# In-projection of a hybrid attention/HGRN2/Fourier layer: the split weights kept in DRAM by the first block of tokens, and one ring of seven buffers

## The chip, the cores and the metric

The kernel runs on one core of one Trainium2 chip. The metric is the device time of one execution in microseconds; lower is better.

## The reference

One layer of a diffusion backbone over 2048 latent tokens and 256 context tokens, width 1024, all in float32:

```python
p = modulate(x, norm1_g[l], sh1, sc1) @ w_in[l]
pc = modulate(ctx, norm1_g[l], csh1, csc1) @ w_in[l]
# columns of p: latent attention (queries, keys/values, rotary key) | HGRN2 (q, two gates, input, output gate) | Fourier
y = jnp.concatenate([attn, hg, fn], axis=-1) @ w_out[l]
x_new = x + g1 * y
x_new = x_new + g2 * swiglu_ffn(modulate(x_new, norm2_g[l], sh2, sc2), w_gate_up[l], w_down[l])
return rms_norm(x, final_norm_g)
```

The change is in the first two lines: the in-projection, a product of the normalised tokens with `w_in` (1024 rows, 2752 columns).

## The kernel before

A product in full precision is made from parts: each operand is split into a high part (a rounded copy in the format float32r) and a low part (the operand less its high part), and three matmuls are added up in PSUM: high by low, high by high, low by high (`mm3`, lines 83 to 85). The helper `hi` makes a high part on POOL (line 72), on ACT (line 74) or on DVE; `lo` makes a low part on DVE (line 79).

The in-projection is the first large stage of the kernel, from about 30 to 895 us. It goes over the context block (256 tokens) and then over four blocks of 512 tokens. In each block, the columns of `w_in` are taken in groups: values and output gate (`values_in`, 512 columns), four heads of the HGRN2 recurrence (`head_in`, 384 columns each: q and two gates), attention (`attention_in`, 448 columns) and Fourier (`fourier_in`, 256 columns). Each group is cut along the 1024 rows into pieces of up to 128 x 1536 elements (`pieces`): three for values, two for each head, three for attention, two for Fourier, 16 in a block of 512 tokens. The context block has 14 pieces with other widths.

For each piece `load_w` loads the raw weights with one DMA on SP's queue per range of columns (line 244; a head's piece has three ranges of 128 columns), makes the high part on POOL (in the context block on ACT) and the low part on DVE, and the matmuls of the piece follow. Raw weights have three buffers (`wraw`), high parts two (`wh`), low parts two (`wl`), each of 128 x 1536 elements. The weights are the same for all blocks, and each block loads and splits them anew.

Between the groups stands the recurrence of each head (`hgrn`): the gates go through ACT (sigmoids, lines 363 and 364, 372), POOL (lines 367, 368, 370, 419), DVE (lines 375, 377, 413, 416) and ACT (copy `ku`, line 387), and PE multiplies small blocks of 128 columns (`psl`, line 392; `pfin`, lines 403 to 410). The gates' results are stored by SP from a ring of two buffers (`gt`), the Fourier part from another of two (`uv`).

The order of the instructions on each engine is laid down when the kernel is built, by the planner of the tile framework, which interleaves the matmuls of the next group with the small matmuls of the recurrence. On the chip each engine and each DMA queue works through its list in order, and waits at an instruction whose input or buffer is not ready.

Of the kernel before, what the change touches and what calls it, by code (L numbers as in the profile page):

```python
# [10 lines left out]
F32 = mybir.dt.float32  # L11
F32R = mybir.dt.float32r
# [7 lines left out]
P = 128  # L20
# [5 lines left out]
TB = 512  # L26
# [16 lines left out]
def tile_backbone(  # L43
# [6 lines left out]
    pe, act, dve, pool, sp = nc.tensor, nc.scalar, nc.vector, nc.gpsimd, nc.sync  # L50

    dram = ctx.enter_context(tc.tile_pool(name="dram", bufs=1, space=DRAM))
# [17 lines left out]
    def hi(eng, dst, src):  # L70
        if eng is pool:
            pool.tensor_scalar(dst, src, 1.0, 0.0, ALU.mult, ALU.add)  # L72
        elif eng is act:
            act.copy(dst, src)  # L74
        else:
            dve.tensor_copy(dst, src)

    def lo(dst, src, h, eng=None):
        (eng or dve).tensor_tensor(dst, src, h, ALU.subtract)  # L79

    def mm3(ps, ah, al, bh, bl, first, last, more=False):

        pe.matmul(ps, ah, bl, start=first, stop=False, skip_group_check=more)  # L83
        pe.matmul(ps, ah, bh, start=False, stop=False, skip_group_check=more)  # L84
        pe.matmul(ps, al, bh, start=False, stop=last, skip_group_check=more)  # L85
# [135 lines left out]
    with p1 as ph:  # L221
        e2 = ph.enter_context(tc.tile_pool(name="p1e2", bufs=2, reuse_waits="tile"))
        ea = ph.enter_context(tc.tile_pool(name="p1ea", bufs=1, reuse_waits="tile"))
        wp = ph.enter_context(tc.tile_pool(name="p1w", bufs=2, reuse_waits="tile"))
# [12 lines left out]
        early = {}  # L237

        def load_raw(cols, n, k0, nk):
            raw = wp.tile([P, 1536], F32, tag="wraw", bufs=3, name="wraw")  # L240
            rv = raw[:, :nk * n].rearrange("p (k n) -> p k n", k=nk)
            o = 0
            for s, wd in cols:
                sp.dma_start(rv[:, :, o:o + wd],
                             w_in[0, k0 * P:(k0 + nk) * P, s:s + wd].rearrange("(k p) n -> p k n", p=P))
                o += wd
            return raw

        def pieces(n):
            step = min(4, 1536 // n)  # L250
            return [(k0, min(step, KT - k0)) for k0 in range(0, KT, step)]

        for k0, nk in pieces(256):
            early[((C_HI, 256), k0)] = load_raw([(C_HI, 256)], 256, k0, nk)
# [4 lines left out]
            state[h] = b2.tile([P, 64], F32, tag=f"S{h}", bufs=6, name=f"S{h}_i")  # L259
            dve.memset(state[h], 0.0)  # L260

        def load_w(cols, n, k0, nk, eng):

            raw = early.pop((cols[0], k0), None)
            if raw is None:
                raw = load_raw(cols, n, k0, nk)
            wh = wp.tile([P, 1536], F32R, tag="wh", name="wh")
            wl = wp.tile([P, 1536], F32R, tag="wl", name="wl")
            hi(eng, wh[:, :nk * n], raw[:, :nk * n])
            lo(wl[:, :nk * n], raw[:, :nk * n], wh[:, :nk * n])  # L270
            return (wh[:, :nk * n].rearrange("p (k n) -> p k n", k=nk),
                    wl[:, :nk * n].rearrange("p (k n) -> p k n", k=nk))

# [44 lines left out]
        def token_major(xm, blk, cols):  # L318
            T = blk[3]
            n = sum(wd for _, wd in cols)  # L320
            acc = [psm.tile([P, 512], F32, tag="mm", name="acc") for _ in range(T // P)]
            for k0, nk in pieces(n):
                wh, wl = load_w(cols, n, k0, nk, pool if T == TB else act)
                for t in range(T // P):
                    for k in range(nk):
                        kk = k0 + k
                        ts = slice(t * P, (t + 1) * P)
                        mm3(acc[t][:, :n], xm[0][kk][:, ts], xm[1][kk][:, ts], wh[:, k, :], wl[:, k, :],
                            kk == 0, kk == KT - 1)
            return acc  # L330

        def feature_major(xm, blk, cols):
            T = blk[3]
            n = sum(wd for _, wd in cols)
            acc = [psm.tile([P, TB], F32, tag="mm", name="accf") for _ in range(n // P)]
            for k0, nk in pieces(n):
                wh, wl = load_w(cols, n, k0, nk, pool if T == TB else act)
                for f in range(n // P):
                    for k in range(nk):
                        kk = k0 + k  # L340
                        fs = slice(f * P, (f + 1) * P)
                        mm3(acc[f][:, :T], wh[:, k, fs], wl[:, k, fs], xm[0][kk][:, :T], xm[1][kk][:, :T],
                            kk == 0, kk == KT - 1)
            return acc
# [110 lines left out]
        def fourier_in(xm, blk):  # L455
            acc = feature_major(xm, blk, [(C_FN, 256)])
            zh = e1.tile([P, 2, TB], F32R, tag="zh", name="zh")
            zl = e1.tile([P, 2, TB], F32R, tag="zl", name="zl")
            for f in range(2):
                hi(act, zh[:, f, :], acc[f])  # L460
                lo(zl[:, f, :], acc[f], zh[:, f, :])
            for t in range(4):
                ts = slice(t * P, (t + 1) * P)
                pu = psm.tile([P, 512], F32, tag="mm", name="pu")
                for f in range(2):
                    mm3(pu, zh[:, f, ts], zl[:, f, ts], cwh[:, f, :], cwl[:, f, :], f == 0, f == 1)
                uv = e1.tile([P, 512], F32, tag="uv", bufs=2, name="uv")
                act.copy(uv, pu)
                sp.dma_start((uva[blk[4]] if blk[4] < NB - 1 else uvz)[t * P:(t + 1) * P, :], uv)

        def attention_in(xm, blk):
            _, w, t0, T, bi = blk
            lat = w == 0
            nt = T // P
            c0 = 0 if lat else C_CKV
            acc = token_major(xm, blk, [(c0, 448 - c0)])
            pt = ea.tile([P, 4, 448], F32, tag="pt", name="pt")
            sq = e2.tile([P, 2, 4], F32, tag="sq", name="sq")
# [70 lines left out]
        def values_in(xm, blk, vp):  # L549
            _, w, t0, T, bi = blk  # L550
            nt = T // P
            acc = token_major(xm, blk, [(C_HI, 512 if w == 0 else 256)])
            vt = vp.tile([P, 4, 256], F32, tag="vt", name="vt")
            for t in range(nt):
                dve.tensor_copy(vt[:, t, :], acc[t][:, 0:256])
                if w == 0:
                    gt = hp[0].tile([P, 256], F32, tag="gt", bufs=2, name="gt")
                    act.activation(gt, acc[t][:, 256:512], AF.Sigmoid)
                    dve.tensor_tensor(gt, acc[t][:, 256:512], gt, ALU.mult)  # L559
                    sp.dma_start(gates[bi][t * P:(t + 1) * P, :], gt)  # L560
            return vt

        def head_in(xm, blk, h):
            cols = [(C_HFF + h * P, P), (C_HFB + h * P, P)]
            if blk[1] == 0:
                cols = [(C_HQ + h * P, P)] + cols
            return feature_major(xm, blk, cols)
# [60 lines left out]
    with ExitStack() as ph:  # L628
# [377 lines left out]
        for b in range(NB):  # L1006
# [19 lines left out]
            if nxt is not None:  # L1026
                _, per_head, heads = nxt
# [10 lines left out]
    with ExitStack() as ph:  # L1038
        wr = ph.enter_context(tc.tile_pool(name="p5w", bufs=2, reuse_waits="tile"))
        wp = ph.enter_context(tc.tile_pool(name="p5p", bufs=9, reuse_waits="tile"))  # L1040
# [272 lines left out]
        for i, (s, j) in enumerate(units):  # L1313
# [4 lines left out]
            for o, n in enumerate(ORDER):  # L1318
# [15 lines left out]
                elif n == 7:  # L1334
                    f = f32("f", 2)
# [61 lines left out]
        for b in range(NB):  # L1397
            sq = b1.tile([P, 4, 2], F32, tag="sq7", bufs=2, name="sq7")
            rs = b1.tile([P, 4, 2], F32, tag="rs7", bufs=2, name="rs7")
            for c in range(2):  # L1400
                acc = [bank("dn") for _ in range(4)]
                for g, (k0, nk) in enumerate(DG):
# [7 lines left out]
                    w = wd.parts.pop(i)  # L1410
# [62 lines left out]
```

## Time and profile before

| what | value |
| --- | --- |
| time, median of 3 runs | 3324.02 us (3322.12 to 3328.81) |
| the profiled execution's own time | 3332.05 us |
| its span, first to last instruction | 3330.3 us |
| PE busy (matmuls) | 3166.0 us, 95% |
| DVE, ACT, POOL busy | 2131.1, 952.4, 1038.6 us |
| moved by DMA | 382.03 MB, 115 GB/s on the mean |

The profiled execution took 3332.05 us, 1.75 us more than its span and 8.0 us more than the median of the three runs. A line of a view names the source line (L79), the engine, the operation, what it writes and reads, and how often it stands there. PE is TensorE's matmuls, DVE VectorE, ACT ScalarE, POOL GpSimd, SP the engine that issues most DMAs.

### The profile page before, as it was taken

The numbers are of one execution on the slowest core, as the hardware profiler recorded it, in microseconds if no ns is written. First come the engines' busy times: TensorE is split into PE (matmuls) and PEld (weight loads), VectorE is DVE, ScalarE is ACT, GpSimd is POOL, SyncE is SP. The second block draws the span as 40 slices with busy tenths as digits, with TensorE's granted clock in tenths as the row PEclk, the third lists the DMA queues.
The fourth block names the chain that finished last, engine by engine and source line by source line (L and its number), as shares of the span: only waits on it lengthen the run. The fifth ranks groups of instructions, "written<-read, shape, count | busy, mean of one in ns | idle before, by whom it ended". The sixth has DMA issues, their size and how long they took to land. (4 is left out here: it accounts for less than half of the span.)

```text
span 3330.3 us, 45440 instructions
## 1 busy us (share of the span) xinstructions
PE 3166.0 (95%) x17034; PEld 2649.5 (80%) x17034; DVE 2131.1 (64%) x3211; ACT 952.4 (29%) x2028; POOL 1038.6 (31%) x1241
## 2 busy tenths in 40 slices
PE   7898989999879999999999989999999999999998
PEld 5777777777668888888888767888878888888886
DVE  6575665646776667676666367766776666555543
ACT  3222121222225555555553241111121111212111
POOL 3443452524430121121001443333333333243442
PEclk9999999999989999999999999999999999999999
DMA  6523233143361112120106665422342232664552
GB/s 228 165 70 124 80 104 92 55 117 102 114 186 34 51 49 79 55 69 26 36 32 228 221 218 161 142 76 86 113 134 80 77 95 92 212 211 155 177 171 70
DMA packets 354000, 382.03 MB, mean 115 GB/s; under 512 B 46234, under 2 KB 236532, under 8 KB 352756
## 3 DMA queue, kind: packets, MB, share of 16 engines
q1 hardware_dynamic: 339140, 368.11, 35.2%
q10 hardware_dynamic: 13776, 8.92, 0.8%
q8 instruction: 135, 2.21, 0.3%
q0 software_dynamic: 864, 2.10, 0.2%
q14 instruction: 85, 0.70, 0.1%
HBM read 293.33 MB, written 85.72 MB: 114 GB/s over the span
## 5 line engine op out<-in xcount | busy, mean ns | idle before, releaser
L72 POOL TENSOR_SCALAR wp<-wr 128x512 fp32r<-128x512 f32 x208 | 170.4, 835 | 354.5 <-PE dn L85 234.0
L890 DVE TENSOR_REDUCE mx<-sc 128x1 f32<-128x512 f32 (+1 forms) x320 | 201.9, 632 | 121.9 <-PE sc L888 121.1
L83 PE MATMUL dn<-wp,hdh 128*128 128x512 f32 x704 | 273.9, 389 | 0.0
L84 PE MATMUL dn<-wp,hdh 128*128 128x512 f32 x704 | 273.9, 389 | 0.0
L85 PE MATMUL dn<-wp,hdl 128*128 128x512 f32 x704 | 273.9, 389 | 0.0
L79 DVE TENSOR_TENSOR wp<-wr,wp 128x512 fp32r<-128x512 f32 x208 | 170.8, 859 | 138.9 <-POOL wp L72 138.7
L79 DVE TENSOR_TENSOR ptl<-ptv,pth 128x512 fp32r<-128x512 f32 x288 | 196.4, 686 | 67.3 <-ACT pth L74 65.0
L74 ACT CAST pth<-ptv 128x512 fp32r<-128x512 f32 x288 | 169.7, 593 | 234.1 <-PE ptv L904 223.7
L896 ACT ACTIVATE p<-sc,mx 128x512 f32<-128x512 f32 (+1 forms) x320 | 201.9, 649 | 91.9 <-DVE mx L893 87.7
L83 PE MATMUL y<-xol,wp 128*128 128x512 f32 x528 | 208.7, 395 | 9.8 <-ACT e L1325 4.6
L72 POOL TENSOR_SCALAR wp<-wg 128x512 fp32r<-128x512 f32 x176 | 131.6, 749 | 269.9 <-PE y L85 107.2
L84 PE MATMUL y<-xoh,wp 128*128 128x512 f32 x528 | 206.9, 392 | 0.0
L85 PE MATMUL y<-xoh,wp 128*128 128x512 f32 x528 | 206.6, 392 | 0.0
L79 DVE TENSOR_TENSOR wl<-wraw,wh 128x1536 fp32r<-128x1536 f32 (+3 forms) x78 | 118.7, 1522 | 119.6 <-POOL wh L72 117.0
L85 PE MATMUL accf<-xh,wl 128*128 128x512 f32 x448 | 184.6, 412 | 10.4 <-DVE wl L79 10.4
L888 PE MATMUL sc<-kth,q 128*128 128x512 f32 (+1 forms) x640 | 194.4, 377 | 0.0
L888 PE MATMUL sc<-kp,q 128*128 128x512 f32 (+1 forms) x640 | 190.0, 373 | 0.0
L83 PE MATMUL accf<-xl,wh 128*128 128x512 f32 x448 | 183.9, 410 | 0.4 <-DVE gt L559 0.4
L84 PE MATMUL accf<-xh,wh 128*128 128x512 f32 x448 | 183.1, 409 | 0.0
L79 DVE TENSOR_TENSOR wp<-wg,wp 128x512 fp32r<-128x512 f32 x176 | 128.5, 733 | 84.6 <-POOL wp L72 80.8
L904 PE MATMUL ptv<-ident,p 128*128 128x128 f32 x1152 | 179.1, 275 | 1.8 <-ACT p L896 1.8
L72 POOL TENSOR_SCALAR wp<-ws 128x512 fp32r<-128x512 f32 x132 | 90.2, 683 | 290.0 <-PE z L85 160.8
(367 smaller groups left out, 8426.4 us busy)
## 6 DMA issues: line engine op xcount, KB each, us to landing
wg<-in_w_gate_up_dram SPq DMA_DIRECT2D x88, 512.0 KB, 4.1
wr<-in_w_down_dram SPq DMA_DIRECT2D x40, 1024.0 KB, 5.3
wraw<-in_w_in_dram SPq DMA_DIRECT2D x112, 256.0 KB, 3.7
hr<-hid SPq DMA_DIRECT2D x88, 256.0 KB, 3.1
wm<-in_w_mod_dram SPq DMA_DIRECT2D x64, 256.0 KB, 2.8
hid<-f SPq DMA_DIRECT2D x44, 256.0 KB, 3.0
hid<-e SPq DMA_DIRECT2D x44, 256.0 KB, 2.0
wt<-in_w_mod_dram SPq DMA_DIRECT2D x8, 1024.0 KB, 7.7
```

The source lines that it names most:

```text
L72: pool.tensor_scalar(dst, src, 1.0, 0.0, ALU.mult, ALU.add)
L74: act.copy(dst, src)
L79: (eng or dve).tensor_tensor(dst, src, h, ALU.subtract)
L83: pe.matmul(ps, ah, bl, start=first, stop=False, skip_group_check=more)
L84: pe.matmul(ps, ah, bh, start=False, stop=False, skip_group_check=more)
L85: pe.matmul(ps, al, bh, start=False, stop=last, skip_group_check=more)
L888: pe.matmul(s[:, :n], a[:, ts], bb[:, js], start=i == 0, stop=i == 4)
L890: dve.tensor_reduce(mx[:, j:j + 1], s[:, :n], AX.X, ALU.max)
L896: act.activation(u["p"][:, a:e], u["s"][i][:, :e - a], AF.Exp, bias=mx[:, 5:6], accum_out=mx[:, 6 + i:7 + i])
L904: pe.transpose(pt[:, i, u * P:(u + 1) * P], ps[u]["p"][:, (2 * g + i) * P:(2 * g + i + 1) * P], ident)
```

## The change

The first block of tokens (T is 512, nothing kept yet) makes both parts of a piece as before and also stores them into two DRAM tensors of its own. The three later blocks load both parts with two DMAs of 128 rows, each row up to 6144 contiguous bytes, and make nothing. The context block has T = 256 and works as before. Raw weights, high parts and low parts share one ring of seven buffers where they had three, two and two of the same size.

```diff
         def load_raw(cols, n, k0, nk):
-            raw = wp.tile([P, 1536], F32, tag="wraw", bufs=3, name="wraw")
+            raw = wp.tile([P, 1536], F32, tag="w", bufs=7, name="wraw")
...
-        def load_w(cols, n, k0, nk, eng):
-
-            raw = early.pop((cols[0], k0), None)
-            if raw is None:
-                raw = load_raw(cols, n, k0, nk)
-            wh = wp.tile([P, 1536], F32R, tag="wh", name="wh")
-            wl = wp.tile([P, 1536], F32R, tag="wl", name="wl")
-            hi(eng, wh[:, :nk * n], raw[:, :nk * n])
-            lo(wl[:, :nk * n], raw[:, :nk * n], wh[:, :nk * n])
+        kept = {}
+
+        def load_w(cols, n, k0, nk, T):
+            at = (cols[0], n, k0)
+            have = kept.get(at)
+            raw = None
+            if have is None:
+                raw = early.pop((cols[0], k0), None)
+                if raw is None:
+                    raw = load_raw(cols, n, k0, nk)
+            wh = wp.tile([P, 1536], F32R, tag="w", bufs=7, name="wh")
+            wl = wp.tile([P, 1536], F32R, tag="w", bufs=7, name="wl")
+            if have is None:
+                hi(pool if T == TB else act, wh[:, :nk * n], raw[:, :nk * n])
+                lo(wl[:, :nk * n], raw[:, :nk * n], wh[:, :nk * n])
+            else:
+                for x, d in zip((wh, wl), have):
+                    sp.dma_start(x.bitcast(F32)[:, :nk * n], d)
+            if have is None and T == TB:
+                kept[at] = [dram.tile([P, nk * n], F32, name=f"w{x}{cols[0][0]}_{k0}") for x in "hl"]
+                for x, d in zip((wh, wl), kept[at]):
+                    sp.dma_start(d, x.bitcast(F32)[:, :nk * n])
```

In `token_major` and `feature_major` the call `load_w(cols, n, k0, nk, pool if T == TB else act)` becomes `load_w(cols, n, k0, nk, T)`.

## Rows read from the trace of the kernel before

**Rows 1.** The page's engines: busy us (share of the span) xinstructions.
```profile
PE 3166.0 (95%) x17034; PEld 2649.5 (80%) x17034; DVE 2131.1 (64%) x3211; ACT 952.4 (29%) x2028; POOL 1038.6 (31%) x1241
```
**Rows 2.** Windows: start, block 0, block 1; the sum is blocks 1 to 3.
```profile
core 0: us, PE busy (x) PEld busy (x) DVE busy (x) ACT busy (x) POOL busy (x), PEclk, DMA share, GB/s
24.00:32.00 8.00, 5.19 (x12) 0.67 (x10) 7.30 (x7) 0.44 (x1) 0.00 (x0) 1.00 0.99 349
105.00:310.00 205.00, 184.17 (x1095) 152.52 (x1094) 134.40 (x176) 57.81 (x121) 91.85 (x88) 0.98 0.41 123
310.00:505.00 195.00, 179.62 (x1105) 148.91 (x1104) 121.48 (x155) 45.90 (x91) 79.03 (x76) 0.97 0.31 91
...
sum 585.00, PE 545.98 PEld 453.08 DVE 361.71 ACT 129.43 POOL 232.31; mean PE 181.99 PEld 151.03 DVE 120.57 ACT 43.14 POOL 77.44
```
**Rows 3.** PE's waits, 310 to 895 us: total us, times, longest.
```profile
PE psl L392 <- ACT ku L387: 16.4, 10, 2.5
PE psl L392 <- DVE q L416: 9.1, 10, 1.8
PE accf L85 <- DVE wl L79: 6.9, 2, 3.5
PE pfin L408 <- DVE q L416: 3.7, 5, 0.9
```
**Rows 4.** Timeline of PE in block 1: start, duration, instruction, [idle before, releaser].
```profile
361.77 1.59 PE L392 MATMUL psl<-q,ku 128*128 128x128 f32 x8 [2.47 <-ACT ku L387]
...
426.28 1.59 PE L392 MATMUL psl<-q,ku 128*128 128x128 f32 x8 [1.54 <-ACT ku L387]
...
484.83 0.50 PE L85 MATMUL accf<-xh,wl 128*128 128x512 f32 x1 [3.46 <-DVE wl L79]
...
499.67 0.71 PE L392 MATMUL psl<-q,ku 128*128 128x128 f32 x3 [1.78 <-DVE q L416]
```
**Rows 5.** Timelines of POOL and (last row) DVE before 426 us.
```profile
415.23 0.77 POOL L367 TENSOR_SCALAR f<-f,omlb,lbt 128x512 f32<-128x512 f32 x1 [9.23 <-ACT f L363]
...
419.35 1.48 POOL L72 TENSOR_SCALAR wh<-wraw 128x1536 fp32r<-128x1536 f32 x1 [2.66 <-PE accf L84]
420.81 2.37 POOL L367 TENSOR_SCALAR f<-f,omlb,lbt 128x512 f32<-128x512 f32 x1
423.26 2.08 POOL L368 TENSOR_SCALAR k<-f 128x1024 f32<-128x1024 f32 x1
...
420.86 1.76 DVE L79 TENSOR_TENSOR wl<-wraw,wh 128x1536 fp32r<-128x1536 f32 x1 [1.37 <-POOL wh L72]
```
**Rows 6.** Timelines of POOL and DVE before 485 and before 500 us.
```profile
475.54 1.06 POOL L72 TENSOR_SCALAR wh<-wraw 128x1024 fp32r<-128x1024 f32 x1 [3.82 <-PE acc L85]
...
483.57 1.21 DVE L79 TENSOR_TENSOR wl<-wraw,wh 128x1024 fp32r<-128x1024 f32 x1
...
495.35 1.91 POOL L72 TENSOR_SCALAR wh<-wraw 128x1536 fp32r<-128x1536 f32 x1
...
494.84 2.96 DVE L79 TENSOR_TENSOR xl<-xmt,xh 128x512 fp32r<-128x512 f32 x2 [0.38 <-POOL xh L72]
```
**Rows 7.** Windows: the 6 us behind PE's stop at 361.77.
```profile
362.00:368.00 6.00, 5.79 (x25) 4.68 (x25) 4.72 (x5) 1.90 (x3) 4.85 (x8) 0.72 0.04 11
```
**Rows 8.** Windows of tile wh alone: what reads or writes it.
```profile
310.00:895.00 585.00, 341.59 (x1056) 198.37 (x1056) 72.94 (x46) 0.00 (x0) 65.44 (x46) 0.98 0.30 88
```
**Rows 9.** DMA issues: KB each, median us to landing.
```profile
wraw<-in_w_in_dram SPq DMA_DIRECT2D x8, 768.0 KB, 4.4
```
**Rows 10.** Timeline of PE: one matmul after another.
```profile
107.62 0.40 PE L83 MATMUL acc<-wl,xh 128*128 128x512 f32 x1
107.85 0.39 PE L84 MATMUL acc<-wh,xh 128*128 128x512 f32 x1
```
**Rows 11.** SP's own waits, 310 to 895 us.
```profile
SPq L244 <- DVE wl L79: 341.5, 33, 19.4
```
**Rows 12.** Windows: the start of block 0.
```profile
105.00:120.00 15.00, 12.31 (x67) 10.04 (x66) 8.68 (x16) 4.41 (x16) 6.28 (x7) 1.00 0.60 164
120.00:140.00 20.00, 19.61 (x87) 15.93 (x86) 12.15 (x18) 7.55 (x15) 7.16 (x7) 1.00 0.95 304
```

More of the change, by code (lines that the diff above doesn't have):

```diff
@@ L322, in token_major @@
             for k0, nk in pieces(n):
-                wh, wl = load_w(cols, n, k0, nk, pool if T == TB else act)
+                wh, wl = load_w(cols, n, k0, nk, T)
                 for t in range(T // P):
@@ L336, in feature_major @@
             for k0, nk in pieces(n):
-                wh, wl = load_w(cols, n, k0, nk, pool if T == TB else act)
+                wh, wl = load_w(cols, n, k0, nk, T)
                 for f in range(n // P):
```

## The prediction

> **What bounds the kernel now.** I read the page's table of engines first. PE is busy 3166.0 of the 3330.3 us, DVE 64%, POOL 31% [rows 1], so an edit pays only where it fills a gap on PE or where PE's clock rises. The change touches the in-projection alone, so I read that stage next, in windows: the context block up to about 105 us, the first block of tokens (block 0) from 105 to 310, blocks 1 to 3 from 310 to 895 [rows 2]. In blocks 1 to 3 PE is busy 545.98 of 585 us. Its idle time there is 39 us: all that can be won there besides the clock. DVE is busy 361.71 us, POOL 232.31, and in block 1 DMA is at 0.31 of its share. So no engine but PE is a bound, and what counts is whose result PE waits for.
>
> PE's waits in those three blocks [rows 3] answer that: 16.4 us for ACT's copy ku, 9.1 + 3.7 for DVE's q, 6.9 for wl, the low part of a weight. Only 6.9 names the removed work. The other waits have to be followed back one engine.
>
> **ku.** PE's longest stop of this kind in block 1 is 2.47 us, and the same stop comes again in blocks 2 and 3 [rows 4]. POOL's timeline before a second stop of the kind, the 1.54 us in rows 4, shows the cause [rows 5]: the sigmoid's L367 takes 0.77 us by itself; the next one stands behind a 1.48 us split of a weight (L72, high part) and itself takes 2.37 us, while DVE makes the low part of that weight (1.76 us, L79). Then POOL's k (2.08), then ACT's ku, then PE. So the split puts 1.48 + (2.37 - 0.77) = 3.08 us into the chain that PE waits for, at the stops of 2.47 and of 1.54 us alike; the ten stops of this kind are 16.4 us.
>
> **wl.** The 3.46 us stop at 484.83, and its twin in block 2 [rows 4]: POOL had the high part done at 476.6, but DVE reached the low part at 483.57, behind the attention part's normalisations [rows 6]. The weight was late only because DVE takes its work in order.
>
> **q.** The 1.78 us stop at 499.67, with a twin in block 2, follows two xl that took 2.96 us together while POOL ran a 1.91 us high part [rows 4, 6]. So 3.6 of the 12.8 us stand behind split work; the other stops are of 1.2 us and less, and I did not follow each.
>
> **The clock.** In the 6 us after the 2.47 us stop the granted clock is 0.72 against 0.97 over the block [rows 2, 7], and PE works at full speed again behind them, so such a stop costs a further 6 x 0.28 = 1.7 us. I take the same for the 3.46 us stops. That makes five (2.47 in each block, 3.46 in two): 8.4 us.
>
> **The change part by part.**
>
> *Removed, blocks 1 to 3:* 16 pieces in each block, so 48 high parts on POOL and 48 low parts on DVE; the trace holds 46 of each, 65.44 and 72.94 us [rows 8]. Neither engine is a bound, so these 138 us count for nothing by themselves; what counts is the waits above. (1) wl: 6.9 us, all of it, because the loaded parts need neither POOL nor DVE. (2) ku: 16.4 us stand behind split work that goes whole. But the instruction order is laid out anew when the kernel is built, and PE's psl will stand earlier once the plan thinks ku earlier; what remains of the chain (k alone is 2.08) can still be late. Bounds 0 and 16.4; I take two thirds, 11. (3) q: bounds 0 and 12.8; 4.5, the 3.6 that were followed back and a little of the rest. (4) Clock: 8.4 if all five stops go, 0 if none; with the two wl stops sure and two thirds of the others, 6. Sum 28.4, bounds 6.9 (wl alone) and 39 + 8.4 = 47 (no idle time left).
>
> On (2) a page can be weighed. Row: the POOL instruction beside DVE's two-input subtraction goes from 0.77 to 2.37 us, and DVE's subtraction is no longer than elsewhere [rows 5]. The Trainium skill (SBUF — State Buffer, Who interferes with whom) has it that a DVE instruction with two SBUF inputs and a GpSimd instruction that reads SBUF exclude each other for a whole instruction. By that, the 1.60 us vanish whole, all 16.4 us go, and the sum would be 5.4 us better; by the row with a new order it is the 11 I keep. The trace agrees with the blocking, though here the instruction that began first was the one held.
>
> *Moved onto DMA, blocks 1 to 3:* per block 2752 columns x 1024 rows x 4 B = 11.3 MB of raw weights become 22.5 MB of two parts. Block 1 moves 91 GB/s x 195 us = 17.7 MB [rows 2]; after, 29 MB, 148 GB/s. The highest rate in these rows is 349 GB/s at a share of 0.99, so the mean fits more than twice over. The number of issues on SP stays: 32 loads for 32 (3 + 4 x 2 x 3 + 3 + 2). A 768 KB load landed in 4.4 us [rows 9]; two for a piece are at most 9 us. With seven buffers and two per piece a load may start when the matmuls four pieces (high part) or three pieces (low part) before are done. A piece of 36 matmuls at 0.23 us is 8.3 us of PE [rows 10], on average 190 / 16 = 12 with the recurrence (the HGRN work of a head). So a load has two pieces, 16 to 24 us, to land in: cost nothing, covered by those matmuls. If that cover were gone it would be 4 us a piece. A load that waits for a buffer holds what stands behind it on SP: gates, mlap, uv and x. SP waits for wl in front of L244 already now, 341.5 us in these blocks [rows 11], without PE stopping for it.
>
> *Added, block 0:* 32 stores, 22.5 MB, on SP. Mean rate 123 GB/s plus 110 = 233, below 349. But from 120 to 140 us the queue is full: 304 GB/s at a share of 0.95 [rows 12]. From 105 to 140 it moves 8.5 MB and could move 12.2; the stores due there are the three pieces of the values (4.2 MB) and the first head piece (1.5). That is 2 MB too much, 6 us until there is room after 140. What waits is the raw load of the first head's second piece and the gate stores, whose two buffers hold ACT and so PE's accumulators. Bounds 0 and 6 + 1.7 of clock; I take 4.5. SP's store also waits for DVE's low part with raw loads behind it; those loads have two pieces to land in, as above.
>
> *The ring, context block and block 0:* a raw weight had a buffer when the low part three pieces earlier was made; now it needs the buffer of the low part three pieces back, so matmuls stand between. The context block's 14 pieces fill the 75 us before 105, 5.4 us each. Load, split and subtraction are at most 4.4 + 1.48 + 1.76 = 7.6 us by rows of larger pieces, against 10.8 us of two pieces: covered on the mean, with little to spare at the start. Bounds 0 and 5; I take 1.5. Behind the stage, the next stage's tiles lie where the ring lay and can be held until the last matmuls: no row here prices that, so 0, with -5 and +5 as an estimate, inside the range.
>
> *Sum:* -28.4 + 4.5 + 1.5 = -22.4. The profiled execution took 3332.05 us, span 3330.3 and 1.75 around; it becomes 3309.6. The median of the three runs is 8.0 lower, 3324.02, so I forecast 3302 there.
>
> **The rivals.**
>
> *All gaps close* (chance 0.07). For it: every long stop in blocks 1 to 3 was traced to split work. Against: k, kd and q still hinder each other on POOL and DVE. -47 + 4 = -43: 3281.
>
> *New waits for old* (0.15). The new order packs PE closer, so that the chain of the recurrence is late again by what the plan does not know, and only wl and its clock are won: -6.9 - 3.4, against 6 to 10 us lost in block 0 and the context: 3320 to 3324. For it: of q's 12.8 us only 3.6 were traced to split work. This is what holds most of "same".
>
> *Slower: the ring gives block 0 only one piece of lead* (0.13). SP keeps its order, so a raw load behind the stores of the piece before waits until that piece's low part is made, then lands behind two stores of some 4.4 us: 3 x 4.4 + 1.5 + 1.76 = 16.5 us after the matmuls that free it, against 8.3 us of PE for a piece with no recurrence beside it. At the six pieces of values and attention that is 6 x 8.2 = 49 us: 3324 - 28 + 49 = 3345. It decides from the point where a raw load has less than two pieces to land. Against it: only two of seven buffers hold a piece that the matmuls are at. Half the effect would end at 3321.
>
> *Bytes for arithmetic does not pay* (0.03). If the weights of blocks 1 to 3 came at the rate of the queue, they would need 29 MB / 349 GB/s = 83 us a block, below the 190 that PE needs, so they cannot bind on the mean. If the 34 MB more were exposed, they would cost 97 us: 3393 with what is won. The Trainium skill (SBUF — State Buffer, A bandwidth-pool intuition that's wrong) says that HBM is almost always the end-to-end bottleneck; the windows of this stage do not show it.
>
> That nothing changes because the parts are made anew each time is excluded: columns, width and first row of a piece are the same in all four blocks, and the context block, which has other widths, keeps nothing.
>
> **How the numbers follow.** My case, -8 to -40, has 0.62, so 3284 to 3316. About 0.2%, 6.6 us, is what a measurement of this kernel can tell from no change. Faster: 0.62 + 0.07 + 0.01 of the new waits = 0.70; same 0.13; slower 0.13 + 0.03 + 0.01 = 0.17. The range runs from the near end of "all gaps close", 3284, to 3328, which takes in new waits and the start of the slower case; outside are some 0.06 below and 0.12 above.
>
> **What would show it.** Right: in blocks 1 to 3 no L72 or L79 on weights, PE's waits for wl gone, those for ku under half, L367 near 0.77 us, PE's granted clock up from 0.97, each block some 8 to 10 us shorter; block 0 longer by a few us with about 230 GB/s. Wrong: PE waiting for a load of wh or wl in blocks 1 to 3, block 0 longer by over 15 us with PE waiting for wl or wraw, or ku waits unchanged though L367 is short.

## The result and the profile after

The changed kernel took 3362.3 us (median of 4 runs, 3356.95 to 3370.6) beside 3325.65 us for the kernel before on the same chip: ratio 1.0109, 95% interval 1.0094 to 1.0124. It is slower by 1.1%, where 0.7% faster was forecast; the time lies above the range. The profiled execution took 3366.77 us, its span is 3365.0 us, 34.7 us more than that of before.

The page's engines of the changed kernel first (busy us, share of the span, instructions; [rows 1] of before):

```profile
PE 3188.9 (95%) x17034; PEld 2668.9 (79%) x17034; DVE 2037.4 (61%) x3163; ACT 950.1 (28%) x2028; POOL 946.7 (28%) x1193
```

The arithmetic is gone as foreseen: DVE lost 93.7 us and POOL 91.9, in 48 instructions each. PE has the same instructions, but is busy 22.9 us longer, at a mean granted clock of 0.971 where before had 0.981.

To find the place of a loss I took two instructions that every block has, and read their first starts in the views by source line: the sigmoid of block 0's output gates on ACT (`gt`), which follows block 0's first group of matmuls (values and output gate), and the copies `uv`, which end each block. Before first, then the changed kernel, where lines stand 15 further down (the gates, then the end of block 0 and the end of block 3):

```profile
L558 ACT ACTIVATE gt<-acc x16: 384/385/387, 131.1 to 735.8; 128x256 f32<-128x256 f32 x16
...
L468 ACT COPY uv<-pu x4: 565/582/587, 304.5 to 308.2; 128x512 f32<-128x512 f32 x4
...
L468 ACT COPY uv<-pu x4: 586/586/591, 893.6 to 899.3; 128x512 f32<-128x512 f32 x4
```
```profile
L573 ACT ACTIVATE gt<-acc x16: 384/385/388, 158.4 to 759.0; 128x256 f32<-128x256 f32 x16
...
L483 ACT COPY uv<-pu x4: 587/588/592, 332.3 to 337.2; 128x512 f32<-128x512 f32 x4
...
L483 ACT COPY uv<-pu x4: 586/586/587, 920.4 to 929.5; 128x512 f32<-128x512 f32 x4
```

The 34.7 us are made up so: 27.3 us are lost before block 0's gates (158.4 against 131.1), 0.5 in the rest of block 0 (173.9 against 173.4), 1.0 is won in blocks 1 to 3 (588.1 against 589.1, from block 0's first `uv` to block 3's), and 7.9 are lost from there to the end (2444.6 against 2436.7). Of the 27.3 us, 21.7 are there at PE's first matmul of block 0 (128.5 us against 106.9).

**Blocks 1 to 3.** Windows of tile wh there (columns as in [rows 2]; [rows 8] of before), then the whole stage, then PE's waits ([rows 3] of before):

```profile
337.00:922.00 585.00, 349.00 (x1056) 202.97 (x1056) 0.00 (x0) 0.00 (x0) 0.00 (x0) 0.95 0.42 142
```
```profile
337.00:922.00 585.00, 551.41 (x3341) 458.54 (x3340) 273.28 (x417) 130.25 (x261) 146.98 (x180) 0.95 0.42 142
```
```profile
PE psl L407 <- ACT ku L402: 15.4, 10, 1.7
PE psl L407 <- DVE q L431: 11.9, 14, 1.6
PE ptx L312 <- ACT xmt L314: 5.3, 2, 2.8
```

No engine splits a weight any more, wl's 6.9 us are gone, and no kept load stands among the waits. But ku kept 15.4 of 16.4 us, q has 11.9 where 12.8 were, a new 5.3 us has come, and the clock of the stretch is 0.95 where three blocks of before had 0.98. Was the chain behind ku not shortened? It was. POOL, PE and the granted clock at the first stop of this kind in block 1 (timelines, then windows; [rows 4, 5, 7] of before):

```profile
380.38 0.77 POOL L382 TENSOR_SCALAR f<-f,omlb,lbt 128x512 f32<-128x512 f32 x1 [1.25 <-ACT f L379]
381.23 2.08 POOL L383 TENSOR_SCALAR k<-f 128x1024 f32<-128x1024 f32 x1
```
```profile
384.24 1.58 PE L407 MATMUL psl<-q,ku 128*128 128x128 f32 x8 [1.66 <-ACT ku L402]
388.38 2.05 PE L407 MATMUL psl<-q,ku 128*128 128x128 f32 x8 [1.06 <-DVE q L431]
418.54 1.57 PE L407 MATMUL psl<-q,ku 128*128 128x128 f32 x8 [1.40 <-ACT ku L402]
422.44 2.05 PE L407 MATMUL psl<-q,ku 128*128 128x128 f32 x8 [0.71 <-DVE q L431]
```
```profile
384.00:390.00 6.00, 4.70 (x19) 3.87 (x20) 4.76 (x4) 1.97 (x4) 5.30 (x8) 0.66 0.12 49
...
418.00:424.00 6.00, 4.74 (x19) 3.85 (x20) 4.98 (x4) 2.27 (x4) 5.55 (x6) 0.67 0.22 90
...
452.00:458.00 6.00, 4.44 (x19) 3.63 (x20) 4.91 (x4) 2.12 (x4) 5.45 (x8) 0.69 0.07 20
```

The first row is what a sigmoid's follow-up costs now: 0.77 us. The view by source line has it for all 24 of them in blocks 1 to 3 (least, median, greatest in ns), where the same view of the kernel before gave 768, 1310 and 2379:

```profile
L382 POOL TENSOR_SCALAR f<-f,omlb,lbt x24: 767/769/814, 377.7 to 895.8; 128x512 f32<-128x512 f32 x24
```

At this stop the last gate's sigmoid starts at 379.68 and PE's psl at 384.24, 4.6 us later; at the 2.47 us stop of [rows 4] it was 355.03 and 361.77, 6.7 us. The chain is 2.2 us shorter. ACT's timelines have this sigmoid at the first and third head of block 1 before, then at the first head now:

```profile
355.03 0.60 ACT L364 ACTIVATE f<-accf 128x512 f32<-128x512 f32 x1 [2.12 <-PE accf L85]
...
419.53 0.60 ACT L364 ACTIVATE f<-accf 128x512 f32<-128x512 f32 x1 [1.30 <-PE accf L85]
```
```profile
379.68 0.60 ACT L379 ACTIVATE f<-accf 128x512 f32<-128x512 f32 x1 [2.12 <-PE accf L85]
```

It is so at nearly every stop for ku: in blocks 1 to 3 the chain took 6.7 us at nine of the ten stops before (5.8 at the last), and takes 4.6 us at all ten now. But PE's list has changed with it. The matmuls of the next group that stand ahead of the first psl of a head are now 13, 14 and 13 in the first three heads of block 1, where they were 19, 14 and 15; between the first and the second psl there are 4, 4 and 4, where there were 6, 4 and 6. A matmul is 0.23 us of cover. In the second and third head, small matmuls of the head before stood in that stretch too (pk and pd, some 2 us; po, 1.7 us), and they now come earlier. The cover, that is the chain less the stop, fell from 4.27, 5.81 and 5.21 us to 2.90, 3.16 and 2.95. So PE's pairs of stops for ku and q in block 1 are 1.66 + 1.06, 1.40 + 0.71 and 1.62 + 1.17 us; in the kernel before they were 2.47 + 0.21, 0.94 alone and 1.54 + 1.18. What the chain gave, the order took. And around each of the three pairs the clock falls (0.66, 0.67 and 0.69 over 6 us), while before it fell at the first alone (0.72 in [rows 7], then 1.00 and 1.00).

**Before block 0's gates.** PE, then POOL, in the changed kernel (timelines):

```profile
113.52 0.53 PE L83 MATMUL acc<-wl,xch 128*128 128x192 f32 x1 [3.48 <-DVE cwl L79]
121.42 0.53 PE L83 MATMUL acc<-wl,xch 128*128 128x192 f32 x1 [5.02 <-DVE cwl L79]
...
142.10 0.66 PE L443 MATMUL pk<-ident,k2c 128*128 128x128 f32 x2 [7.14 <-DVE k2c L428]
```
```profile
117.50 1.47 POOL L72 TENSOR_SCALAR wh<-wraw 128x1536 fp32r<-128x1536 f32 x1 [7.82 <-DMA wraw<-in_w_in_dram]
128.43 1.49 POOL L72 TENSOR_SCALAR wh<-wraw 128x1536 fp32r<-128x1536 f32 x1 [9.46 <-DMA wraw<-in_w_in_dram]
...
137.49 1.04 POOL L72 TENSOR_SCALAR wh<-wraw 128x1024 fp32r<-128x1024 f32 x1 [4.36 <-DMA wraw<-in_w_in_dram]
```

The three pieces of block 0's values are split at 117.5, 128.4 and 137.5 us, each as soon as its raw weights land. Before, POOL split the first two at 103.44 and 106.12 and waited for no raw weight. The late splits hold what stands behind them in order: DVE's low part of the first piece (119.00) stands ahead of the context block's cwl, so PE waits 5.02 us for cwl; DVE's low part of the third piece (138.56) stands ahead of the last steps of k2c, so PE waits 7.14 us for a head of the context block. Why the weights are late stands in SP's own waits, 24 to 140 us; the first row has no counterpart in the kernel before, where SP waited in front of L244 for DVE and not for matmuls:

```profile
SPq L244 <- PE accf L85: 27.3, 7, 7.3
SPq L244 <- DVE wl L79: 23.5, 9, 5.2
```

### The profile page after: what moved, and what is told of

The parts are those of the page before. It is cut to its first block, busy times and chain, and to the rows that moved or that the text cites. A ratio compares the mean times of both kernels' runs of the same rounds, so it can differ in the third digit from the quotient of the medians.

```text
span 3365.0 us, 45397 instructions
## 1 busy us (share of the span) xinstructions
PE 3188.9 (95%) x17034; PEld 2668.9 (79%) x17034; DVE 2037.4 (61%) x3163; ACT 950.1 (28%) x2028; POOL 946.7 (28%) x1193
## 5 line engine op out<-in xcount | busy, mean ns | idle before, releaser
L79 DVE TENSOR_TENSOR wp<-wg,wp 128x512 fp32r<-128x512 f32 x176 | 128.4, 732 | 85.4 <-POOL wp L72 81.9
L83 PE MATMUL po<-ptl,ckh 128*128 128x256 f32 x576 | 169.7, 295 | 0.0
```

## The experiments

All marks below are first starts in the profiled execution, in us; "ratio" is to the kernel before on the same chip, with its 95% interval.

| run | time | ratio | gates, block 0 | uv, block 0 | blocks 1 to 3 | from there to the end |
| --- | --- | --- | --- | --- | --- | --- |
| before | | 1 | 131.1 | 304.5 | 589.1 | 2436.7 |
| the change | 3362.3 | 1.0109 (1.0094 to 1.0124) | 158.4 | 332.3 | 588.1 | 2444.6 |
| e1, ring only | 3379.4 | 1.0158 (1.0140 to 1.0176) | 157.7 | 338.4 | 606.7 | 2434.6 |
| e2, keeping only | 3338.6 | 1.0038 (1.0025 to 1.0051) | 132.3 | 310.1 | 588.2 | 2439.6 |
| e3, high part only | 3330.6 | 1.0007 (0.9995 to 1.0019) | 127.0 | 302.4 | 581.2 | 2438.0 |
| e4, stores only | 3336.4 | 1.0032 (1.0020 to 1.0044) | 129.6 | 311.2 | 586.9 | 2430.6 |
| e6, e2 with more buffers | 3336.9 | 1.0019 (1.0006 to 1.0031) | 130.1 | 307.4 | 584.8 | 2442.1 |
| e7, e2 with products later | 3336.1 | 1.0027 (1.0017 to 1.0036) | 133.7 | 311.5 | 574.9 | 2446.1 |
| e8, before with products later | 3332.3 | 1.0012 (1.0003 to 1.0022) | 128.6 | 302.4 | 585.1 | 2443.4 |
| e10, the change, raw weights ahead | 3334.2 | 1.0023 (1.0010 to 1.0036) | 136.0 | 312.8 | 580.4 | 2437.1 |
| e11, e10 with both edges | 3304.2 | 0.9938 (0.9921 to 0.9955) | 135.9 | 313.4 | 543.7 | 2443.1 |
| e12, before with both edges | 3316.7 | 0.9963 (0.9947 to 0.9979) | 128.5 | 303.4 | 568.9 | 2444.5 |
| e14, e11 with edges in block 0 too | 3305.7 | 0.9939 (0.9924 to 0.9954) | 136.7 | 312.0 | 544.6 | 2444.4 |
| e15, e2 with both edges | 3305.5 | 0.9933 (0.9916 to 0.9949) | 133.6 | 308.3 | 549.2 | 2444.6 |

The marks of a row come from one execution, and executions of one kernel differ: the ten of e10 took 3323.2 to 3342.5 us, at mean granted clocks of 0.984 to 0.975. Differences of some us between two marks, or up to about 8 us in the last column, are therefore not shown to belong to the kernels; the large ones (27 us before the gates, 20 us and more in blocks 1 to 3) go with waits that are there or gone in the traces.

**The change taken apart.** e1 is the kernel before with the ring of seven alone, e2 the changed kernel with the three rings of before:

```diff
-            raw = wp.tile([P, 1536], F32, tag="wraw", bufs=3, name="wraw")
+            raw = wp.tile([P, 1536], F32, tag="w", bufs=7, name="wraw")
...
-            wh = wp.tile([P, 1536], F32R, tag="wh", name="wh")
-            wl = wp.tile([P, 1536], F32R, tag="wl", name="wl")
+            wh = wp.tile([P, 1536], F32R, tag="w", bufs=7, name="wh")
+            wl = wp.tile([P, 1536], F32R, tag="w", bufs=7, name="wl")
```

e2 takes these lines of the change back and leaves the rest.

> The kernel before, with raw weights, high parts and low parts in one ring of seven buffers; nothing is kept. Theory R (the ring delays the raw loads of the context block and of the start of block 0): slower than before by 20 to 30 us, nearly all of it gained before PE's first matmul of block 0, which the changed kernel starts at 128.5 instead of 106.9 us. Theory S (the 22.5 MB of stores fill the queue and SP's order in block 0): within 5 us of before.

> The change with the three rings of before (three raw, two high, two low). Theory R: the context block ends at 105 to 108 us as before, and the whole is within 10 us of before, on either side. Theory S: block 0 still loses 15 to 25 us, so the whole is 15 to 30 us slower than before. Theory P (in blocks 1 to 3 the planner puts psl earlier and PE waits for ku as often): in blocks 1 to 3 PE still waits 12 to 17 us for ku and the blocks are within 3 us of before together.

The gates come at 157.7 us with the ring alone and at 132.3 with the keeping alone: the 27 us before the gates are the ring's. The gates in the views by source line, e1 first:

```profile
L558 ACT ACTIVATE gt<-acc x16: 383/384/387, 157.7 to 779.6; 128x256 f32<-128x256 f32 x16
```
```profile
L573 ACT ACTIVATE gt<-acc x16: 383/383/386, 132.3 to 733.9; 128x256 f32<-128x256 f32 x16
```

Where nothing is kept, the ring goes on costing: 7.3 us in block 0 and 17.6 in blocks 1 to 3, so that e1 is 53 us slower and not theory R's 20 to 30; what costs there was not followed. Without the ring, the change still loses 0.4%, 12 us, between theories R (10 at most) and S (15 at least), and blocks 1 to 3 again gain about 1 us, as theory P had it.

In e3 the later blocks load the high part alone and use it as both parts, so the low part is left out of their products; it halves the loads and the stores. e4 is the kernel before with the stores of both parts in block 0, which nobody reads.

```diff
+            at = (cols[0], n, k0)
+            if eng is pool and at in kept:
+                one = wp.tile([P, 1536], F32R, tag="wraw", bufs=3, name="wone")
+                sp.dma_start(one.bitcast(F32)[:, :nk * n], kept[at])
+                ov = one[:, :nk * n].rearrange("p (k n) -> p k n", k=nk)
+                return ov, ov
```

> Three rings; only the high part is kept, and blocks 1 to 3 load it once and use it as high and as low part, so they neither split nor load more bytes than before; the product lacks its low part there. Stores are half. Theory P: the ku waits of blocks 1 to 3 stay at 12 to 17 us and the blocks gain less than 5 us together, though nothing of DMA is added. If DMA is what ate the gain, blocks 1 to 3 gain 15 to 30 us together.

> The kernel before, with the stores of both parts added in block 0; blocks 1 to 3 load and split as before, three rings. Theory S: slower than before by 15 to 25 us, in block 0. Theory R: slower by 0 to 6 us, the context block unchanged.

The stores cost block 0, from its gates to its first uv, 181.6 - 173.4 = 8.2 us in e4 and 177.8 - 173.4 = 4.4 in e2; e4 is 9.9 us slower in all, between theory R's 6 and theory S's 15. With half the bytes blocks 1 to 3 took 7 us less (581.2 against 588.2), 7.9 less than before, where theory P allowed 5 and the rival asked for 15; the stops stayed as they were, ku 15.5 and q 15.4 us. e10, below, takes 580.4 us there with all the bytes. So bytes are not what holds the later blocks.

**More room for the kept pieces.** In e6 every third kept piece goes to two of the raw buffers, idle by then.

```diff
+            late = kept_turn[0] % 3 == 2 if have is not None else False
+            wh = wp.tile([P, 1536], F32R, tag="wraw" if late else "wh", bufs=3 if late else 2, name="wh")
+            wl = wp.tile([P, 1536], F32R, tag="wraw" if late else "wl", bufs=3 if late else 2, name="wl")
+            kept_turn[0] += have is not None
```

> Both parts kept, three rings as before (3338.6 us), but in the three later blocks every third kept piece lands in two of the buffers that the raw weights no longer need, so three pieces can be ahead where two were. Theory (the loads of kept pieces come in time; TensorE waited 1.7 us in all for them in the run with three rings): no change, 3336 to 3341 us. Rival (what keeps the later blocks from gaining is that loads of 1.5 MB a piece crowd the two buffers): 3325 to 3332 us, with the first uv copies of blocks 0 and 3 under 582 us apart, where 588.2 were.

3336.9 us, as the theory had it; the waits for ku and q are 15.5 and 14.5 us. The kept loads are not late.

**The order of the products.** e7 takes e2 and puts, in blocks 1 to 3, a head's first psl behind matmul 22 of the next group and its second behind 36; e8 puts the kernel before at 30 and 44. The edges change no data, only the order that is laid down when the kernel is built (`pend` holds the two products of a head with these numbers, `done` the matmuls of the next group; the lines that fill them are left out here):

```diff
+        def behind(done):
+            for psl, at in pend:
+                tc.add_manual_dep(psl.ins, done[at - 1].ins.name,
+                                  mybir.DependencyInfo(mybir.DependencyClass.NoSync, mybir.DependencyReason.DATA),
+                                  reason="psl behind the next group's matmuls")
+            pend.clear()
```

> Both parts kept, three rings, and in blocks 1 to 3 the first within-chunk product of a head (psl) is put behind 22 matmuls of the next group instead of 13, the second behind 36 instead of 17. Theory (the order laid out anew gave the saved time back as a second stop for each head): TensorE's waits for ku and q in blocks 1 to 3, 15.5 and 13.4 us with three rings, fall together under 12 us, the stage's clock rises from .96 to .97 or .98, the first uv copies of blocks 0 and 3 are 570 to 580 us apart instead of 588, and the time is 3320 to 3331 us. Rival (the stops only move on to the next wait for q, masks or buffers): the two waits keep their sum or others grow by as much, 3335 to 3342 us.

> The kernel before, nothing kept, with the same order put on it: the first product behind 30 matmuls of the next group instead of 19, the second behind 44. It tells what the order is worth without the change. Theory: the splits' hold on VectorE and GpSimd makes the chain longer and uneven, so the waits (ku 16.4, q 9.1 us) fall but not all, and wl's 6.9 us stay: 3313 to 3321 us, that is less gain than the same order gives where the parts are kept. Rival (the order alone was the limit, and the splits cost nothing but their own waits): as much gain as in the other run or more, under 3313 us.

PE's waits in e7, 316 to 900 us:

```profile
PE po L479 <- DVE S L471: 18.0, 9, 2.2
PE ptx L312 <- ACT xmt L314: 6.8, 4, 2.7
PE psl L420 <- DVE q L446: 3.5, 7, 0.7
```

Both theories were half right. The waits for ku and q fell from 28.9 to 3.5 us and blocks 1 to 3 by 13.3 us, but a wait of 18.0 us under a new name took over: DVE now worked on the next head (q, kd and k, 5 us) ahead of this head's states S, for which PE's po waits. And the stretch after the stage took 6.5 us more than in e2, which may be no more than the difference between executions; the time, 3336.1 us, shows no gain. e8 has 4.0 us less in blocks 1 to 3, with ku's wait gone, q's up from 9.1 to 14.6 and po's from 1.4 to 6.4; its 3332.3 us are no gain either, and miss the theory's 3313 to 3321.

**The lead of the raw weights.** e10 is the changed kernel, ring and all, but the raw weights of a piece take their buffer ahead of the parts of the piece before them. The ring then hands a raw weight the buffer that the low part four pieces back held, not three. (`groups`, left out here, lists the column groups of the context block and block 0 in their order.)

```diff
+        ahead = [(c, sum(wd for _, wd in c), k0, nk) for c in groups for k0, nk in pieces(sum(wd for _, wd in c))][1:]
...
                 raw = early.pop((cols[0], k0), None)
-                if raw is None:
-                    raw = load_raw(cols, n, k0, nk)
+                if ahead:
+                    c, m, j0, nj = ahead.pop(0)
+                    if (c[0], j0) not in early:
+                        early[(c[0], j0)] = load_raw(c, m, j0, nj)
```

> The changed kernel, one ring of seven, with one difference: the raw weights of a piece take their buffer one piece earlier (before the parts of the piece ahead of them), so a raw load waits for the matmuls of the piece four before it instead of three. Theory (the 27 us that the ring cost before block 0's gates are the lead of the raw loads): the first copy of block 0's gates comes at 130 to 140 us instead of 158.4, GpSimd's wait for raw weights falls from 21.6 us to under 8, and the time to 3335 to 3347 us. Rival (seven buffers in one ring are too few whatever the order, or the parts are what comes late): gates still after 150 us, 3354 us or more.

POOL's splits of block 0's values in e10 (timeline; the changed kernel's stand above):

```profile
101.02 1.47 POOL L72 TENSOR_SCALAR wh<-wraw 128x1536 fp32r<-128x1536 f32 x1 [4.45 <-DVE wl L79]
106.89 1.47 POOL L72 TENSOR_SCALAR wh<-wraw 128x1536 fp32r<-128x1536 f32 x1 [4.40 <-DVE wl L79]
112.96 1.06 POOL L72 TENSOR_SCALAR wh<-wraw 128x1024 fp32r<-128x1024 f32 x1 [4.59 <-issue]
```

This one change of order in the ring gives back 28.1 us of the 36.7: 3334.2 us, just under the theory's range. The gates come at 136.0, the splits 16 to 25 us sooner, and none waits for a raw weight. SP still waits 26.1 us for acc and 23.4 for accf in front of L244, but a piece sooner, where it holds nobody. So it is the lead that cost, not the number of buffers. In blocks 1 to 3 PE's list has the same order as in the changed kernel, as far as the records of the two traces show, and as many stops (ten for ku, 15.5 us, and fourteen for q, 15.0 us where the changed kernel had 11.9), yet the stage took 580.4 us instead of 588.1, at a clock of 0.98 instead of 0.95. This run also has 2437.1 us after block 3, as before: the 7.9 us that the changed kernel has more there are not shown to come from the ring.

**Both edges.** e11 is e10 with the products behind 22 and 38 matmuls, and with the next head's kd on DVE behind this head's S. e12 puts the same on the kernel before (30 and 46), e14 extends e11 to block 0.

```diff
+                if bi >= 1 and h > 0:
+                    tc.add_manual_dep(one.ins, last_s[0].ins.name,
+                                      mybir.DependencyInfo(mybir.DependencyClass.NoSync, mybir.DependencyReason.DATA),
+                                      reason="kd behind the head before's states")
```

> The ring with raw weights one piece ahead (3334.2 us), with two kinds of edges in blocks 1 to 3: the first product of a head behind 22 matmuls of the next group, the second behind 38, and the next head's kd on VectorE only after this head's states S. In the run with the first kind alone, TensorE's waits for ku and q fell from 28.9 to 3.5 us and a new wait of 18.0 us for S came. Theory (each stop is only an order in which something stands too early, and taking out the third one pays): po's wait for S under 5 us with ku and q under 8, first uv copies of blocks 0 and 3 558 to 570 us apart (580.4 with the ring alone), 3314 to 3326 us. Rival (the chain of a head through GpSimd and VectorE is as long as the group that hides it, so every edge moves the stop on): waits of 15 us or more under another name, 572 us or more apart, 3328 to 3338 us.

> The kernel before with both kinds of edges in blocks 1 to 3 (products behind 30 and 46 matmuls, kd after S); nothing kept, the splits still there. Theory (the splits lengthen the chain unevenly, so the edges help less): 578 to 585 us between the first uv copies of blocks 0 and 3 (585.1 with the first kind alone), wl's 6.9 us still there, 3322 to 3332 us. Rival (order alone was the limit): under 572 us and under 3320 us, as much as where the parts are kept.

> The same as the ring with raw weights ahead and both kinds of edges, with the edges in block 0 too, where the splits and the stores still run. Theory (block 0 has the same second stop of a head): its gates to its first uv copy shrink from 176.8 us by 3 to 8 us, 3308 to 3322 us. Rival (in block 0 other waits end last: raw weights, stores, GpSimd): no difference to the edges in blocks 1 to 3 alone, within 3 us.

Blocks 1 to 3 of e11: the window, PE's waits in it, and the 12 us around the first two products of a head:

```profile
318.00:857.00 539.00, 523.06 (x3269) 439.22 (x3268) 263.23 (x408) 130.32 (x262) 143.30 (x180) 1.00 0.46 156
```
```profile
PE ptx L319 <- ACT xmt L321: 8.3, 6, 2.7
PE pfin L450 <- DVE q L458: 3.2, 7, 0.5
PE psl L432 <- DVE q L458: 2.2, 7, 0.4
```
```profile
366.00:372.00 6.00, 5.78 (x31) 4.73 (x30) 4.32 (x5) 2.13 (x4) 4.38 (x7) 1.00 0.26 53
372.00:378.00 6.00, 6.00 (x35) 4.86 (x34) 5.18 (x9) 1.50 (x3) 0.00 (x0) 1.00 0.52 210
```

And PE's waits in blocks 1 to 3 of e12, 308 to 872 us:

```profile
PE psl L410 <- DVE q L436: 13.5, 17, 2.2
PE accf L85 <- DVE wl L79: 6.8, 2, 3.4
PE pfin L428 <- DVE q L436: 6.4, 9, 0.9
```

With both edges, ku is gone from the waits, po's S is 0.4 us, and the stage runs at a clock of 1.00. Blocks 1 to 3 take 543.7 us, less than the theory's 558 to 570, and the time is 3304.2 us, less than its 3314 to 3326. The same edges take the kernel before to 568.9 us and 3316.7 us, better than the theory's 578 to 585 and 3322 to 3332, and inside what the rival asked for (under 572 and under 3320), though not as much as where the parts are kept: the order alone was worth 20.2 us in blocks 1 to 3. What the keeping is worth there, with these edges in both, is 568.9 - 543.7 = 25.2 us (19.7 with three rings, e15). What remains in e12 is q and wl: wl's 6.8 us are a split's, and before the longest stop for q, 2.19 us at 371.56, DVE made a low part from 368.45 on. Whether other numbers of matmuls than 30 and 46 would suit the kernel before still better was not tried. Over the whole kernel the keeping is worth 3316.7 - 3304.2 = 12.5 us, with intervals that overlap a little; e14 and e15 keep the parts too and take 3305.7 and 3305.5 us. Of the 25.2 us, 10.0 are paid back by the end of block 0 (its uv at 313.4 against 303.4), 7.4 of them before its gates. The edges in block 0 add nothing (e14), as the rival had it.

**Whether the ring is worth anything.**

> Both parts kept, three rings as in the kernel before, and both kinds of edges in blocks 1 to 3 (products behind 22 and 38 matmuls, kd after the states S). It tells whether the one ring is worth anything once its lead and the order are mended (3304.2 us with it). Theory (TensorE hardly waits for a kept piece, 1.7 us with three rings, so two buffers a part are enough): first uv copies of blocks 0 and 3 545 to 552 us apart (546.7 with the ring) and 3302 to 3311 us. Rival (seven shared buffers let the kept pieces come further ahead, and that pays once the stops are gone): over 556 us apart with waits for wh or wl of 5 us or more, 3312 us or more.

e15 is e2 with e11's edges: 3305.5 us and 0.9933 (0.9916 to 0.9949), the same as with the ring. Its waits for kept loads are 1.7 us in all. Two buffers a part are enough. (The 546.7 us that its text gives for the ring is misread: the first uv of block 3 in e11 starts at 857.1 us, so it is 543.7.)

## Why the prediction was wrong

Two steps failed, and a rival with a small chance had come near each. In the span of the profiled execution 22.4 us of gain were forecast and 34.7 us of loss measured, 57 us apart: some 26 of them are the ring's and 27 those of blocks 1 to 3.

*The ring, taken at 1.5 us with bounds 0 and 5*: measured 27.3 us, the largest error and the one that gives the sign. The step compared 7.6 us of load, split and subtraction with "two pieces, 10.8 us", from 14 pieces that fill 75 us on the mean. The 7.6 was about right, 7.9: a load issued at 112.9 in the changed kernel is split at 117.50 and subtracted by 120.8. The mean of the pieces was the wrong cover. The pieces at the end of the context block are 192 columns wide, and behind them comes the first piece of values itself, with no matmuls of block 0 there yet to hide it. Nor does the delay stay with the piece, since POOL and DVE take the context block's own k2c and cwl in order behind the late split. The rival "the ring gives block 0 only one piece of lead" (0.13, 3345 us) came nearest to the mechanism, a raw load that starts too late, but put it at the stores and at the pieces of block 0; it struck at the change from the context block to block 0, and without any stores (e1). "Only two of seven buffers hold a piece that the matmuls are at" was beside the point: a ring hands out its buffers in order, so the one that comes next counts, not how many are free. e10 settles it.

*ku, q and the clock, 11 + 4.5 + 6 of the 28.4 us*: about 1 us came of the whole sum in blocks 1 to 3 (588.1 against 589.1; 588.2 in e2, and 8.7 us in e10, the best of the four with this order). The reading of the rows was right in kind: the sigmoid's follow-up is never held any more, 767 to 814 ns in all 24 cases. It was too large in size: the split put 2.2 us into the chain, not 3.08. In [rows 5] the split runs from 419.35, but the sigmoid that the follow-up needs ends only at 420.13 (419.53 + 0.60), so some 0.6 of the 1.48 us count. The Trainium skill (SBUF — State Buffer, Who interferes with whom) has the follow-up and the subtraction exclude each other, by which the 1.60 us would go whole; the duration bears this out. The 16.4 us that the prediction tied to it did not go. What failed is the two thirds: "psl will stand earlier once the plan thinks ku earlier" was written as a bound and then priced at a third of the wait. Over the ten stops the chain became about 21 us shorter, more than the whole wait of 16.4, but the cover in front of psl fell by about 20 us, and 15.4 us of waiting stayed. The sum of q's stops stayed about as it was. The prediction had named this among the signs that it would be wrong: ku's waits unchanged though L367 is short. The clock, 6 us of gain forecast, fell from 0.98 to 0.95 in the changed kernel; with the same order in e2, e6 and e10 it was 0.96, 0.97 and 0.98, and the stage 588.2, 584.8 and 580.4 us. That is the rival "new waits for old" (0.15). The 25.2 us of e11 against e12 show that nearly the 28.4 were there to be had once the order was set by hand. e11 stands 45.4 us below before in these blocks, close to the 47 of "all gaps close", but 20.2 of them are the order's, which the change did not touch.

*wl, 6.9 us*: right as to the wait, which is gone in every run that keeps the parts. Its time was not seen in the stage's length, because the other stops and the clock took it.

*Block 0's stores, 4.5 us*: 4.4 us in e2, 8.2 in e4, which is a little over the upper bound of 7.7, and 0.5 in the changed kernel itself, whose stage starts late. The executions differ too much to tell these apart.

*Loads of kept parts, 0*: right; PE waited 1.7 us in e2 and neither more buffers (e6 beside e2) nor the ring of seven beside three rings (e11 beside e15) made a difference in the time.

*The next stage, 0 with 5 either way*: 7.9 us in the changed kernel. There POOL waits 12.7 us with its DMA into wpeh for the last matmuls on a weight, as feared; but e10, with the same ring, waits 9.1 us at a later one of these DMAs and ends as early as before. Over all runs this stretch varies from 2430.6 to 2446.1 us. Whole executions of one kernel differ by as much, so it is not shown that the change costs anything there; what sets it stays open.

## What to carry to other kernels

Putting several rings into one does not only pool the buffers, it ties the order of release: work out for each tile whose buffer it takes over, and what has to finish first, at the narrowest pieces and at the change from one loop to the next, not on the mean. When work is removed from a chain that a planner has scheduled, ask how long the chain is against the cover that the new order will give it; a wait that survives with a shorter chain is an order to be set by hand, and only after it is set can the removal be judged.

## What the runs showed of the hardware

Stops of TensorE of the same size do not always cost clock. The pair of 1.54 and 1.18 us in the kernel before, at 426.28 and 430.43, was passed at a granted clock of 1.00 in the windows around it; the pair of 1.62 and 1.17 us in the changed kernel, at 452.39 and 456.53, at 0.69 and then 0.58, most of the stretch at the lower of the two levels (1.2 of 2.4 GHz). One window of each, before first:

```profile
426.00:432.00 6.00, 4.54 (x25) 3.88 (x26) 5.14 (x5) 2.12 (x4) 5.34 (x8) 1.00 0.00 1
```
```profile
456.00:462.00 6.00, 5.47 (x22) 4.87 (x23) 2.92 (x5) 1.58 (x3) 1.68 (x5) 0.58 0.00 0
```

What decides between the two was not found. It need not lie in the kernel: ten executions of e10, one program, have mean granted clocks from 0.975 to 0.984, and of these the two at the ends took 3340.15 and 3323.22 us. The 7.7 us by which blocks 1 to 3 differ between the changed kernel and e10, with as many stops on PE, are of that size. With nearly no stops the clock stayed up: in e11, with 0.22 us left at such a place, it is 1.00, and 1.00 over the three blocks. From e10 to e11 PE's three longest waits fell from 36.0 to 13.7 us, 22.3 us less, and the blocks became 36.7 us shorter; a clock of 1.00 for 0.98 over some 580 us is about 12 of the rest.
